# A hybrid decoder trunk: the first LRU input chunk of each layer is worked in two token halves, the first of them between the two halves of V

## The chip, the cores and the metric

The kernel runs on one core of one Trainium2 chip. The metric is the device time in microseconds (us) of one execution; the time before is 1116.06 us, the median of three runs. TensorE (PE) multiplies, VectorE (DVE) and ScalarE (ACT) do the element-wise work, GpSimd (POOL) some small operations and transfers, and SyncE (SP) issues most of the transfers from memory. PEld is TensorE's weight load, which a profile lists apart from the multiplication itself.

## The reference, cut to what matters

There are 256 tokens of width 1024, and two layers. Each layer is

```
h = RMSNorm_pre(x)
[q | k | v | lru_x | lru_gate | glu_in | branch_gates] = h @ w_in
A = dilated attention(q, k, v) @ w_o_attn
B = (RG-LRU(causal_conv4(lru_x)) * gelu(lru_gate)) @ w_o_lru
C = swish(LayerNorm(causal_conv31(GLU(glu_in)))) @ w_o_conv
x += RMSNorm_post((sigmoid-gated sum of A, B, C) @ w_out)
x += RMSNorm_post(relu(RMSNorm_pre(x) @ w_up)^2 @ w_down)
```

All of it is in float32. What the change touches is the product of `h` with 256 of the 1024 columns of `lru_x` (the chunk called lx1) in each layer, and where that product stands beside the product for the first third of V.

## The kernel before, in words

**Weights.** All weights come in chunks of 1 MB (128 partitions x 2048 floats), 92 for each layer, in a fixed order (ORDER and chunk_plan). The function `weights` loads a chunk into a raw buffer (two of them, tag "raw"), then splits it in two pieces of 1024 columns: ACT casts to `whi`, rounded to the type fp32r (line 416), and DVE subtracts to get the rest, `wlo` (line 429). `whi` and `wlo` have three buffers each. The activations are split likewise, into `hh` and `hl`. A product is then three fp32r matmuls for each block of 128 input rows: whi*hh, whi*hl and wlo*hh.

**Two forms of product.** In the form "ws" the weights are the stationary operand (128x128) and the tokens stream past, all 256 of them: `ws_items` makes, for each half j of a chunk and each four blocks k, a list a of eight matmuls (whi) and a list b of four (wlo), that is 48 matmuls of 256 columns for a chunk. In the form "as" the activations are stationary and 512 weight columns stream past; one matmul makes 128 tokens. V is in this form: two chunks (v00, v01), and for each 128 tokens t 12 matmuls of 512 columns for each chunk.

**The start of a layer.** `h` is made in two token halves: `pre_norm(t)` squares and sums on ACT, finds the root, scales on DVE (`xn_mix`), transposes on PE (`pt_mix`, line 483) and splits into `hh_mix` (ACT) and `hl_mix` (DVE). The first entry of ORDER, v0, is therefore taken apart (`vproj` with apart true): first both chunks for the tokens t=0, then both for t=1. The second entry is lx1, the third glu0. At the start of layer 1 the last matmuls of the layer before (`dn`) for t=1 stand between.

**What sets the order.** Every operation is an `Op`; `main` chains all products in the order in which the program makes them, so PE works them in that order, with transposes and the small products of attention put between them. A planner (`Sched.run`) simulates the five engines with a cost for each operation, takes the ready one with the longest way to the end, and fixes the order of the instructions on every engine. For an fp32r matmul the cost it uses is 0.4266 ns for each streamed column. The engines then run their lists in order and wait on each other. PSUM accumulators of the tag "mm" have four places, and each chunk's matmuls wait for their accumulator, for `whi`/`wlo` and for `hh`/`hl`.

**After lx1.** `lx` copies the accumulator (`xp`), makes a causal convolution of four taps over all 256 tokens (`lu`) and splits it; that is used some chunks later by `lru_gates`. The loads of the LRU gate weights (`lwr`, POOL's queue) are ordered behind `starts["lx1"]`.

Of the kernel before, what the change touches and what calls it, by code (L numbers as in the profile page):

```python
# [13 lines left out]
P = 128  # L14
T = 256
# [361 lines left out]
def trunk_kernel(ctx: ExitStack, tc: tile.TileContext, x_d, pos_d, w_d, lruw_d, par_d, gain_d, const_d, id_d, out_d):  # L377
# [5 lines left out]
    S = Sched()  # L383
# [4 lines left out]
    def slot(name, dt=F32, shape=(P, 2, T)):  # L388
        return S.buf(sp, shape, dt, "s2", name, NSLOT)

    def mm_ps(name, shape=(P, 2, T), ring=True):
        return S.buf(pp, shape, F32, "mm", name, 4, ring)
# [55 lines left out]
    def dma(eng, out, in_, nbytes):  # L448
        def fn():
            o = out.ap() if isinstance(out, View) else out  # L450
            i = in_.ap() if isinstance(in_, View) else in_
            eng.dma_start(out=o, in_=i)

        e = {id(nc.gpsimd): "POOL", id(nc.scalar): "ACT"}.get(id(eng), "SP")
        o = S.op(e, DMA_ISSUE[e], fn, views(in_), views(out))
        o.dma = nbytes / DMA_RATE / 1e3
        return o

    def memset(out, v):
        return S.op("POOL", 60 + 0.5 * out.n, lambda: nc.gpsimd.memset(out.ap(), v), [], [out])  # L460

    def matmuls(items):
        cost = 0
        reads, writes, seen = [], [], set()
        for out, lhs, rhs, start, stop in items:
            n = rhs.n
            cost += n * 0.4266 if lhs.buf.dt == F32R else n * 1.69
            for v, l in ((lhs, reads), (rhs, reads), (out, writes)):
                k = (id(v.buf), v.reg, l is writes)
                if k not in seen:  # L470
                    seen.add(k)
                    l.append(v)

        def fn():
            for out, lhs, rhs, start, stop in items:
                nc.tensor.matmul(out.ap(), lhsT=lhs.ap(), rhs=rhs.ap(), start=start, stop=stop)  # L476

        return S.op("PE", cost, fn, reads, writes)
# [8 lines left out]
    last_main = [None]  # L487

    def main(items, *more):
        for it in (items,) + more:  # L490
            o = matmuls(it)
            o.main = True
            if last_main[0] is not None:
                S.follow(last_main[0], o)
            last_main[0] = o
        return o

    def split(hi, lo, src, scale=None):
        if scale is None:
            return act(hi, src, AF.Copy), tt(lo, src, hi.f32(), OP.subtract)  # L500
        return (act(hi, src, AF.Copy, scale=scale),
                stt(lo, src, scale, hi.f32(), OP.mult, OP.subtract))
# [5 lines left out]
    def weights(l, name, spread=False):  # L508
        c = CIDX[name]
        assert c == used[l], (name, c, used[l])  # L510
        used[l] += 1
        nm = f"{name}_{l}"
        raw = S.buf(wp, (P, CHUNK), F32, "raw", f"raw_{nm}", NRAW)
        if l or c:
            o = dma(nc.sync, raw.all(), w_d[l * NCH + c], CHUNK * P * 4)
            if l == 0 and c in late:
                S.follow(o, late[c])
        else:
            for s in range(2):
                o = dma(nc.sync, raw[:, s * HALF:(s + 1) * HALF], w_d[0][:, s * HALF:(s + 1) * HALF], HALF * P * 4)  # L520
                if ORDER[0][0] == "v":
                    S.follow(o, x1_load)
        if spread:
            hs, ls = [], []
            for q in range(4):
                hs.append(slot(f"whi_{nm}{q}", F32R, (P, 512)))
                ls.append(slot(f"wlo_{nm}{q}", F32R, (P, 512)))
                for o in split(hs[q].all(), ls[q].all(), raw[:, q * 512:(q + 1) * 512]):
                    o.prep = True
            return [(Quarters(hs[2 * s:2 * s + 2]), Quarters(ls[2 * s:2 * s + 2])) for s in range(2)]  # L530
        offs = (3 * LINE // 8, LINE // 8) if KIND[name] != "as" else (3 * LINE // 8,) * 2 if name[:2] in ("v1", "v2") else (0, 0)
        hi = Shifted(S.buf(wp, (P, CHUNK + LINE // 2), F32R, "whi", f"whi_{nm}", NHI), offs[0])
        lo = Shifted(S.buf(wp, (P, CHUNK + LINE // 2), F32R, "wlo", f"wlo_{nm}", NHI), offs[1])
        n = HALF if l == 0 and c < 2 else PREP
        for b in range(0, CHUNK, n):
            for o in split(hi[:, b:b + n], lo[:, b:b + n], raw[:, b:b + n]):
                o.prep = True
        return [(Part(hi, s * HALF), Part(lo, s * HALF)) for s in range(2)]
# [30 lines left out]
    def alloc_h(name):  # L569
        hi = [S.buf(sp, (P, 4, T), F32R, "hh", f"hh_{name}_{b}", 2) for b in range(2)]  # L570
        lo = [S.buf(sp, (P, 4, T), F32R, "hl", f"hl_{name}_{b}", 2) for b in range(2)]
        return hi, lo
# [56 lines left out]
    def hk(h, k, sl=slice(None)):  # L629
        return h[0][k // 4][:, k % 4, sl], h[1][k // 4][:, k % 4, sl]  # L630
# [90 lines left out]
    rope_tables()  # L721
    softplus()

    def ws_items(ps, j, w, rhs, nk=8, pitch=P, off=0):
        hi, lo = w
        out = []
        for k0 in range(0, nk, 4):
            a, b = [], []
            for k in range(k0, k0 + 4):
                s = slice(k * pitch + off, k * pitch + off + P)  # L730
                mh, ml = rhs(k)
                a.append((ps[:, j, :], hi[:, s], mh, k == 0, False))
                a.append((ps[:, j, :], hi[:, s], ml, False, False))
                b.append((ps[:, j, :], lo[:, s], mh, False, k == nk - 1))
            out += [a, b]
        return out

    def ws_mm(ps, w, rhs):
        first = last_main[0]
        for j in range(2):  # L740
            main(*ws_items(ps, j, w[j], rhs))

    for l in range(L):
        if l == 0:
            h = h0
        hr = lambda k, h=h: hk(h, k)
# [4 lines left out]
            late[6] = last_gain[0]  # L751
        merged = {}
        upad, cacc, taps = {}, {}, {}
        starts = {}

        def gemm(name, w, ps, rhs):
            n0 = len(S.ops)
            ws_mm(ps, w, rhs)
            starts[name] = S.ops[n0]

        def p1(buf, i):
            return buf[:, l, i:i + 1]
# [44 lines left out]
        lu, luh, lul, lru = {}, {}, {}, {}  # L807

        def lx(j):
            w = weights(l, f"lx{j}")  # L810
            ps = mm_ps(f"lx{j}_{l}")
            gemm(f"lx{j}", w, ps, hr)
            xp = S.buf(sp, (P, 2, 260), F32, "xp", f"xp{j}_{l}", 2)
            memset(xp[:, :, 0:3], 0.0)
            act(xp[:, :, 3:3 + T], ps.all(), AF.Copy)
            u = slot(f"lu{j}_{l}")
            for s in range(2):
                i = 2 * j + s
                act(u[:, s, :], ps[:, s, :], AF.Identity, scale=p1(par, CW + 24 + i), bias=p1(par, CB + i))
            for k in range(3):  # L820
                for s in range(2):
                    i = 2 * j + s
                    stt(u[:, s, :], xp[:, s, k:k + T], p1(par, CW + k * 8 + i), u[:, s, :], OP.mult, OP.add)
            lu[j] = u
            luh[j] = slot(f"luh{j}_{l}", F32R)
            lul[j] = slot(f"lul{j}_{l}", F32R)
            split(luh[j].all(), lul[j].all(), u.all())
# [83 lines left out]
        def vproj(g, apart):  # L911
            acc = [mm_ps(f"v{g}{t}_{l}", (P, 512)) for t in range(2)]
            src = lambda kk, t: hk(h, kk, slice(t, T, 2) if g else slice(t * P, (t + 1) * P))
            ws = [weights(l, f"v{g}0")] + ([weights(l, f"v{g}1")] if apart else [])

            def part(kb, t):
                if len(ws) <= kb:
                    ws.append(weights(l, f"v{g}{kb}"))
                for q in range(2):
                    m = main(as_items(acc, ws[kb][q], src, (4 * kb + 2 * q, 4 * kb + 2 * q + 1), 7, t))  # L920
                    starts.setdefault(f"v{g}", m)

            for t in ((0,), (1,)) if apart else ((0, 1),):
                for kb in range(2):
                    part(kb, t)
            for t in range(2):
                vt[g, t] = slot(f"vt{g}{t}_{l}", shape=(P, 512))
                act(vt[g, t].all(), acc[t].all(), AF.Copy)
# [160 lines left out]
        mh, ml = {}, {}  # L1089
# [23 lines left out]
        for name in ORDER:  # L1113
            kind, a = name[:2], name[2:]
# [39 lines left out]
        h = alloc_h(f"mlp{l}")  # L1154
# [30 lines left out]
        hr = lambda k, h=h: hk(h, k)  # L1185
# [37 lines left out]
        for kb in range(1, 8):  # L1223
# [4 lines left out]
            for c in range(2):  # L1228
                w = weights(l, f"dn{kb - 1}{c}", HOLD and kb == 7 and c == 1 and l + 1 < L)
# [7 lines left out]
        if l + 1 < L:  # L1237
            h = alloc_h(f"mix{l + 1}")
# [108 lines left out]
```

## Time and profile before

| | |
|---|---|
| median of three runs | 1116.06 us (1115.8 to 1116.9) |
| the profiled execution | 1113.95 us, of which the span of the trace is 1112.2 us |
| matmuls | 8258 |
| DVE, ACT, POOL busy | 81%, 65%, 6% of the span |
| granted TensorE clock, mean | 0.999 |
| memory traffic | 201.08 MB read, 182 GB/s over the span |

In the rows below all times are in us from the start of the span, unless marked ns. A row of the timeline gives the start, the length, the engine, the line, the operation with output and inputs, the shapes and a count; in brackets stands the idle time before it with what ended that. Matmuls overlap in the pipeline: the record of one is longer than the distance to the next one, and the distance from start to start is what a matmul costs in a stream. Where a row holds x4, its length is three distances and one record.

### The profile page before, as it was taken

To read this page: it belongs to the slowest core of one execution; us is meant where nothing else is said; L and a number is where in the kernel's file an instruction comes from. 1 tells how busy PE (TensorE), PEld (TensorE's weight loads), DVE (VectorE), ACT (ScalarE), POOL (GpSimd) and SP (SyncE) were. 2 spreads that over 40 slices of the span, in tenths; PEclk is the share of its full clock that TensorE was granted. 3 is DMA by queue.
4 is the path that set the end of the run, shared out by engine and by line. 5 is a ranking of instruction groups with operands and counts; after the bars stand their busy time and mean duration, and the time that the engine had idled before them with its cause. 6 is when DMAs were issued, how large, how long until landed. Compare 5 with 4: busy or idle time off the path is not lost.

```text
span 1112.2 us, 20605 instructions
## 1 busy us (share of the span) xinstructions
PE 1095.9 (99%) x8258; PEld 1023.9 (92%) x8258; DVE 902.4 (81%) x1380; ACT 727.7 (65%) x1186; POOL 70.1 (6%) x156
## 2 busy tenths in 40 slices
PE   7999999999999999999999999999999999999997
PEld 6999999998899899989889999999988998998996
DVE  6999999999969865555679999999996889655554
ACT  5879948787775454444569896569676746444443
POOL 1000022111000110000000000221200001000000
PEclk9999999999999999999999999999999999999999
DMA  8664466554436565555555553764633364555551
GB/s 294 247 208 152 152 226 236 184 193 149 142 121 245 195 211 197 194 194 189 189 200 215 181 182 116 255 222 171 216 123 143 146 248 161 214 190 189 194 190 71
DMA packets 37650, 209.77 MB, mean 189 GB/s; under 512 B 6449, under 2 KB 9777, under 8 KB 14130
## 3 DMA queue, kind: packets, MB, share of 16 engines
q1 hardware_dynamic: 32976, 200.05, 50.9%
q0 software_dynamic: 4576, 8.40, 2.3%
q8 instruction: 65, 1.06, 0.4%
q14 instruction: 31, 0.25, 0.1%
q10 hardware_dynamic: 2, 0.00, 0.0%
HBM read 201.08 MB, written 1.05 MB: 182 GB/s over the span
## 4 chain that ended last, share of the span: by engine, by line
PE 82%; DVE 10%; ACT 4%; DMA 2%; issue 1%; SPq 0%; DVEq 0%; ACTq 0%
PE dn L476 15%; PE up L476 14%; PE glu L476 8%; PE v L476 6%; PE ga L476 4%; PE gc L476 4%; PE wo L476 4%; PE oc L476 4%; PE lx L476 3%; PE k L476 3%; PE q L476 3%; PE lg L476 2%; PE ob L476 2%; PE ua L476 2%; PE oa L476 2%; PE pv L476 1%
## 5 line engine op out<-in xcount | busy, mean ns | idle before, releaser
L429 DVE TENSOR_TENSOR wlo_dn<-raw_dn,whi_dn 128x1024 fp32r<-128x1024 f32 (+1 forms) x66 | 76.7, 1190 | 71.2 <-ACT whi_dn L416 71.2
L416 ACT CAST whi_dn<-raw_dn 128x1024 fp32r<-128x1024 f32 (+1 forms) x66 | 65.4, 1023 | 78.9 <-PE dn L476 41.0
L433 DVE SCALAR_TENSOR_TENSOR c<-upad,parh,c 128x256 f32<-128x256 f32 x256 | 110.6, 477 | 0.1
L476 PE MATMUL up<-hl_mlp,whi_up 128*128 128x256 f32 x448 | 107.9, 277 | 0.0
L476 PE MATMUL up<-hh_mlp,whi_up 128*128 128x256 f32 x448 | 107.9, 277 | 0.0
L429 DVE TENSOR_TENSOR wlo_up<-raw_up,whi_up 128x1024 fp32r<-128x1024 f32 x56 | 67.3, 1222 | 48.2 <-ACT whi_up L416 48.2
L476 PE MATMUL dn<-whi_dn,uh 128*128 128x512 f32 x256 | 99.8, 390 | 0.0
L476 PE MATMUL dn<-wlo_dn,uh 128*128 128x512 f32 x256 | 99.8, 390 | 0.0
L423 ACT ACTIVATE cpd<-upad,parh 128x256 f32<-128x256 f32 x224 | 95.3, 499 | 5.7 <-DVE c L429 5.1
L416 ACT CAST whi_up<-raw_up 128x1024 fp32r<-128x1024 f32 x56 | 57.1, 1047 | 51.7 <-PE dn L476 25.4
L476 PEld LDWEIGHTS up<-hh_mlp,whi_up 128*128 128x128 f32 x448 | 84.1, 188 | 0.5
L476 PEld LDWEIGHTS up<-hl_mlp,whi_up 128*128 128x128 f32 x448 | 84.1, 188 | 0.5
L476 PE MATMUL dn<-whi_dn,ul 128*128 128x512 f32 x256 | 70.0, 389 | 0.0
L476 PE MATMUL up<-hh_mlp,wlo_up 128*128 128x256 f32 x448 | 69.4, 277 | 0.0
L429 DVE TENSOR_TENSOR cpd<-cpd 128x1024 f32<-128x1024 f32 (+2 forms) x84 | 63.0, 773 | 0.3 <-ACT cpd L423 0.3
L476 PE MATMUL glu<-hh_mix,whi_glu 128*128 128x256 f32 x256 | 61.2, 276 | 0.0
L476 PE MATMUL glu<-hl_mix,whi_glu 128*128 128x256 f32 x256 | 61.2, 276 | 0.0
L476 PEld LDWEIGHTS up<-hh_mlp,wlo_up 128*128 128x128 f32 x448 | 59.4, 188 | 0.0
L476 PEld LDWEIGHTS dn<-whi_dn,ul 128*128 128x128 f32 x256 | 48.1, 188 | 10.0
L476 PEld LDWEIGHTS dn<-wlo_dn,uh 128*128 128x128 f32 x256 | 48.1, 188 | 9.6
L476 PEld LDWEIGHTS dn<-whi_dn,uh 128*128 128x128 f32 x256 | 48.1, 188 | 9.5
L476 PEld LDWEIGHTS glu<-hl_mix,whi_glu 128*128 128x128 f32 x256 | 48.1, 188 | 0.0
(309 smaller groups left out, 3446.6 us busy)
## 6 DMA issues: line engine op xcount, KB each, us to landing
raw_dn<-w_in_stream SPq DMA_DIRECT2D x32, 1024.0 KB, 4.8
raw_up<-w_in_stream SPq DMA_DIRECT2D x28, 1024.0 KB, 4.8
raw_glu<-w_in_stream SPq DMA_DIRECT2D x16, 1024.0 KB, 4.9
raw_q<-w_in_stream SPq DMA_DIRECT2D x12, 1024.0 KB, 5.0
raw_k<-w_in_stream SPq DMA_DIRECT2D x12, 1024.0 KB, 4.8
raw_v<-w_in_stream SPq DMA_DIRECT2D x11, 1024.0 KB, 4.9
raw_lx<-w_in_stream SPq DMA_DIRECT2D x8, 1024.0 KB, 4.8
raw_lg<-w_in_stream SPq DMA_DIRECT2D x8, 1024.0 KB, 4.8
```

Of the source, the lines that this page charges most:

```text
L416: nc.scalar.copy(out.ap(), in_.ap())
L423: nc.scalar.activation(out.ap(), in_.ap(), func, scale=val(scale), **kw)
L429: lambda: nc.vector.tensor_tensor(out=out.ap(), in0=a.ap(), in1=b.ap(), op=op), [a, b], [out])
L433: lambda: nc.vector.scalar_tensor_tensor(out=out.ap(), in0=a.ap(), scalar=val(s), in1=b.ap(), op0=op0, op1=op1), [a, b] + views(s), [out])
L476: nc.tensor.matmul(out.ap(), lhsT=lhs.ap(), rhs=rhs.ap(), start=start, stop=stop)
```

## The change: what it does

`ws_items` takes a range of token columns, `cols`. A new function, `ws_part`, makes the products of a chunk for the 128 tokens of half t only: the same 48 matmuls (24 for each j), each with 128 streamed columns in place of 256. In `vproj`, when v0 is taken apart, the weights and the accumulator of lx1 are fetched after the V matmuls for t=0, and `ws_part` for t=0 is put there; the V matmuls for t=1 follow. Where `lx(1)` stood, `ws_part` for t=1 takes the place of the whole product, into the same accumulator. `starts["lx1"]` is now the first operation of the first half. The order of the chunks in memory and of their loads stays. The planner's cost of a matmul of 128 columns is half that of one of 256.

```diff
--- before.py
+++ after.py
@@ -721,7 +721,7 @@
     rope_tables()
     softplus()
 
-    def ws_items(ps, j, w, rhs, nk=8, pitch=P, off=0):
+    def ws_items(ps, j, w, rhs, nk=8, pitch=P, off=0, cols=slice(0, T)):
         hi, lo = w
         out = []
         for k0 in range(0, nk, 4):
@@ -729,16 +729,20 @@
             for k in range(k0, k0 + 4):
                 s = slice(k * pitch + off, k * pitch + off + P)
                 mh, ml = rhs(k)
-                a.append((ps[:, j, :], hi[:, s], mh, k == 0, False))
-                a.append((ps[:, j, :], hi[:, s], ml, False, False))
-                b.append((ps[:, j, :], lo[:, s], mh, False, k == nk - 1))
+                a.append((ps[:, j, cols], hi[:, s], mh, k == 0, False))
+                a.append((ps[:, j, cols], hi[:, s], ml, False, False))
+                b.append((ps[:, j, cols], lo[:, s], mh, False, k == nk - 1))
             out += [a, b]
         return out
 
     def ws_mm(ps, w, rhs):
-        first = last_main[0]
         for j in range(2):
             main(*ws_items(ps, j, w[j], rhs))
+
+    def ws_part(ps, w, h, t):
+        cols = slice(t * P, (t + 1) * P)
+        for j in range(2):
+            main(*ws_items(ps, j, w[j], lambda k: hk(h, k, cols), cols=cols))
 
     for l in range(L):
         if l == 0:
@@ -751,7 +755,7 @@
             late[6] = last_gain[0]
         merged = {}
         upad, cacc, taps = {}, {}, {}
-        starts = {}
+        starts, ahead = {}, {}
 
         def gemm(name, w, ps, rhs):
             n0 = len(S.ops)
@@ -807,9 +811,13 @@
         lu, luh, lul, lru = {}, {}, {}, {}
 
         def lx(j):
-            w = weights(l, f"lx{j}")
-            ps = mm_ps(f"lx{j}_{l}")
-            gemm(f"lx{j}", w, ps, hr)
+            if f"lx{j}" in ahead:
+                w, ps = ahead[f"lx{j}"]
+                ws_part(ps, w, h, 1)
+            else:
+                w = weights(l, f"lx{j}")
+                ps = mm_ps(f"lx{j}_{l}")
+                gemm(f"lx{j}", w, ps, hr)
             xp = S.buf(sp, (P, 2, 260), F32, "xp", f"xp{j}_{l}", 2)
             memset(xp[:, :, 0:3], 0.0)
             act(xp[:, :, 3:3 + T], ps.all(), AF.Copy)
@@ -923,6 +931,11 @@
             for t in ((0,), (1,)) if apart else ((0, 1),):
                 for kb in range(2):
                     part(kb, t)
+                if t == (0,):
+                    ahead["lx1"] = weights(l, "lx1"), mm_ps(f"lx1_{l}")
+                    n0 = len(S.ops)
+                    ws_part(ahead["lx1"][1], ahead["lx1"][0], h, 0)
+                    starts["lx1"] = S.ops[n0]
             for t in range(2):
                 vt[g, t] = slot(f"vt{g}{t}_{l}", shape=(P, 512))
                 act(vt[g, t].all(), acc[t].all(), AF.Copy)
```

## Rows read from the trace of the kernel before

**Rows 1.** The page: busy time by engine, and the granted clock in 40 slices.
```profile
PE 1095.9 (99%) x8258; PEld 1023.9 (92%) x8258; DVE 902.4 (81%) x1380; ACT 727.7 (65%) x1186; POOL 70.1 (6%) x156
...
PEclk9999999999999999999999999999999999999999
```
**Rows 2.** The chain that ended last, in order of time: start, us, what.
```profile
16.55 8.20 PE v L476 x36
24.74 5.47 PE lx L476 x48
...
566.18 5.82 PE v L476 x24
572.00 5.47 PE lx L476 x48
```
**Rows 3.** Timeline of PE, start of layer 1.
```profile
559.87 0.73 PE L476 MATMUL v<-whi_v,hl_mix 128*128 128x512 f32 x2 [0.32 <-DVE hl_mix L429]
...
564.09 0.61 PE L476 MATMUL v<-whi_v,hl_mix 128*128 128x512 f32 x2
564.88 1.29 PE L483 MATMUL pt_mix<-ident,xn_mix 128*128 128x128 f32 x8 [0.17 <-DVE xn_mix L433]
```
**Rows 4.** Instructions of tile lx: duration ns min/median/max, first and last start.
```profile
L476 PEld LDWEIGHTS lx<-hh_mix,whi_lx x128: 187/188/188, 24.4 to 636.4; 128*128 128x128 f32 x128
L476 PE MATMUL lx<-hh_mix,whi_lx x128: 276/276/280, 24.6 to 636.5; 128*128 128x256 f32 x128
```
**Rows 5.** Timeline of PEld and PE (last row: by tile, ns): short matmuls with 128-column loads.
```profile
311.78 0.53 PEld L476 LDWEIGHTS var<-ones,vars 128*128 128x128 f32 x4
311.90 0.50 PE L476 MATMUL var<-ones,vars 128*128 128x1 f32 x4
...
556.21 0.60 PE L483 MATMUL pt_mix<-ident,xn_mix 128*128 128x128 f32 x4
...
L483 PE MATMUL pt_mix<-ident,xn_mix x32: 270/273/475, 7.1 to 565.9; 128*128 128x128 f32 x32
```
**Rows 6.** Instructions by tile: weight loads of 32 and of 64 columns.
```profile
L476 PEld LDWEIGHTS mup<-c,ones x32: 106/108/109, 296.5 to 849.2; 128*32 128x32 f32 x32
...
L476 PEld LDWEIGHTS pv<-pT,vt x192: 132/137/137, 266.6 to 847.2; 128*64 128x64 f32 x192
```
**Rows 7.** Timeline of layer 0 by engine: end of V for t=0, and lx1's weights.
```profile
18.69 0.61 PE L476 MATMUL v<-whi_v,hl_mix 128*128 128x512 f32 x2
...
17.49 1.98 ACT L416 CAST whi_lx<-raw_lx 128x1024 fp32r<-128x1024 f32 x2
...
18.71 0.28 DVE L690 CAST rt_r<-posi 128x256 f32<-128x256 int32 x1
...
19.29 2.29 DVE L429 TENSOR_TENSOR wlo_lx<-raw_lx,whi_lx 128x1024 fp32r<-128x1024 f32 x2
```
**Rows 8.** Timeline of DVE, layer 1: weights of lx1 and of glu0.
```profile
565.31 1.22 DVE L429 TENSOR_TENSOR wlo_lx<-raw_lx,whi_lx 128x1024 fp32r<-128x1024 f32 x1
...
570.40 2.36 DVE L429 TENSOR_TENSOR wlo_glu<-raw_glu,whi_glu 128x1024 fp32r<-128x1024 f32 x2 [2.67 <-ACT whi_glu L416]
```
**Rows 9.** Waits of PE, whole span: us in total, times, longest.
```profile
PE sc L476 <- DVE mx L972: 2.2, 2, 1.4
...
PE tp L483 <- ACT sm L423: 0.5, 1, 0.5
PE psi L476 <- ACT lu L423: 0.5, 2, 0.3
```
**Rows 10.** Instructions of tile rt_r: rope-table operations on DVE in layer 0.
```profile
L433 DVE SCALAR_TENSOR_TENSOR rt_r<-rt_nh,rt_r x6: 415/418/419, 32.4 to 58.5; 128x256 f32<-128x256 f32 x6
```
**Rows 11.** Timeline of PE: the attention product, with 64-column loads.
```profile
266.59 1.96 PE L476 MATMUL pv<-pT,vt 128*64 128x256 f32 x24
```
**Rows 12.** Instructions of tile mu: a matmul of plain f32.
```profile
L476 PE MATMUL mu<-mus,ones x4: 377/378/378, 302.9 to 851.4; 128*128 128x256 f32 x4
```
**Rows 13.** Timeline of PE, layer 0: V just after the engine's first work.
```profile
12.23 1.05 PE L476 MATMUL v<-whi_v,hl_mix 128*128 128x512 f32 x2
```

## The prediction

> **What bounds the kernel now.** I read the busy times first: TensorE is busy for 1095.9 of 1112.2 us, and no other engine comes near [rows 1]. So an instruction more on TensorE is paid in full unless it fills time in which TensorE waited. Then I read the chain that ended last around the two places of the change. In layer 0 it is TensorE's own: 36 V matmuls in 8.20 us (0.228 us each) and then the 48 of lx1 in 5.47 us (0.114 each) [rows 2]. In layer 1 it is the same pair, behind the norm of the last tokens [rows 2]. The third view is TensorE's timeline at the start of layer 1, for what the change could win. The reader is to see how little idle time there is. The last two V matmuls for t=0 start at 564.09, so TensorE could take the next instruction at 564.09 + 2 x 0.228 = 564.55. The eight transposes of the other token half start at 564.88, since xn_mix was late: 0.33 us lost [rows 3]. At 0.11 us each (worked out below) they are through at 565.75, and V for t=1 starts at 566.18 [rows 2], when the split of the transposed half is there: 0.43 us lost. That is 0.76 us in all, and the 0.32 us before them [rows 3] lie inside V for t=0, ahead of what is moved. In layer 0 V runs from t=0 into t=1 in one stretch of 36 matmuls without a break [rows 2]: there is nothing to win.
>
> **The price of the split.** The change keeps the number of streamed columns (48 x 256 = 2 x 48 x 128) and doubles the matmuls: 96 for lx1 in each layer, each with its own weight load, 96 more in the whole program. So everything hangs on the distance between two fp32r matmuls of 128 columns with 128x128 loads, and no row has one. I bound it from both sides.
>
> From below: if only the columns counted, half of 0.114, that is 0.057 us, and the split would cost nothing. From above: if a matmul this short were worked like plain f32. The plain f32 matmul of 256 columns has two instructions to a matmul, and each record is 378 ns [rows 12] where one of fp32r is 276 [rows 4]; the 102 ns more are about another 256 columns at 0.114 us. So a plain f32 matmul streams each column four times, and 128 columns would take 4 x 0.057 = 0.228 us.
>
> Nearest lies a third figure, the weight load. A load's record grows with its columns: 108 ns for 32, 137 for 64 [rows 6], 188 for 128 [rows 4], that is 80 ns for (188 - 108) / 96 = 0.83 ns a column, in which 128 columns take 107 ns. That this is a rate and not only a delay is seen where matmuls are too short to cover it. The var matmuls stream one column each, yet their four loads stand in 0.53 us, (0.53 - 0.19) / 3 = 0.113 us apart [rows 5]; the matmuls follow at the same distance. The transposes have 128 columns and 128-column loads, as the new matmuls will, and four stand in 0.60 us with a record of 0.273: (0.60 - 0.273) / 3 = 0.109 us [rows 5]. So at 256 columns load and stream just balance, and at 128 the load sets the pace. I take 0.114 us, what lx has today: 96 x 0.114 = 10.94 us for lx1 in place of 5.47, so **+5.47 us in each layer, +10.9 us in all**.
>
> The Trainium skill speaks of this distance too ("TensorE: Matmul & The Clock Gate", section "Back-to-back issue gap"): a sustained stream of load and matmul pairs is given there as about 81 ns a matmul at 128 columns. By that the cost would be 96 x 0.081 - 5.47 = 2.3 us a layer. The same sentence gives about 131 ns at 512 columns, where this trace has 228 [rows 2], so I don't follow it here.
>
> **What the change wins or waits for, layer 1.** Half of lx1 now covers the time until hh_mix and hl_mix for t=1 are there, 5.47 us against the 1.6 us from 564.55 to 566.18; V for t=1 will not wait. The transposes still have to stand among the lx1 matmuls; if they are put a list too early, TensorE waits for xn_mix as now. I take 0.6 of the 0.76 us. lx1's own weights are late next: its second j needs the last wlo_lx piece after 24 + 8 matmuls, at 564.55 + 32 x 0.114 = 568.2, and that piece ends at 565.31 + 1.22 = 566.53 even where it stands today [rows 8]. If it moves ahead of the norm on DVE, the norm is later by 1.2 us, inside the cover of 5.47.
>
> **Layer 0.** V for t=0 ends at 18.69 + 2 x 0.228 = 19.15 [rows 7], and lx1 starts 5.4 us earlier than before. Its first eight matmuls need whi_lx alone, whose first half is ready at 18.5; they end at 20.06. The next four need the first half of wlo_lx, which today starts at 19.29 and ends at about 20.45 [rows 7]: a wait of 0.4 us. It is in nobody's way but TensorE's, behind it are V for t=1 and all the rest. The planner may put that subtraction ahead of the conversion at 18.71 and the small operations behind it, and the wait goes; if it stays behind the other split, it is up to 1 us. I take 0.4.
>
> **What else moves.** No transfer is added. glu0's weights need the buffers of v00, which come free after the first twelve V matmuls for t=1, now 5.47 us later. Until glu0 starts there are twelve V matmuls and half of lx1, 2.7 + 5.5 us as before, so the 4.7 us between the end of wlo_glu (570.40 + 2.36 = 572.76) and glu0's start at 572.00 + 5.47 = 577.47 remain [rows 2, 8]. The raw loads behind it on SP's queue shift with TensorE. The lwr loads on POOL's queue are only ordered behind an earlier operation, and are needed after further chunks. The accumulator of lx1 is held for some 11 us more; of the four places two are V's. I cost these at nothing; the cover is that 4.7 us.
>
> **What is given back later.** TensorE's 5.47 us more at the start of layer 0 are time in which DVE can do rope-table work; six such operations of 0.42 us, 2.5 us, stand later, between 32 and 59 [rows 10]. The waits of TensorE for DVE and ACT later come to 2.2 + 0.5 + 0.5 = 3.2 us in both layers [rows 9]. In layer 1 DVE has no such work to bring forward: its preparation is tied to weight buffers that TensorE frees later too. I take 1.0 us given back, in layer 0; bounds 0 and 3.2.
>
> **The sum.** 10.9 - 0.6 + 0.4 - 1.0 = +9.7 us. Against the profiled execution that is 1113.95 + 9.7 = 1123.7; its span is 1112.2, with 1.75 us around it that the change leaves alone. The median of the runs lies 2.1 us above that execution, so I forecast 1116.06 + 9.7 = **1125.8 us**. Its own range is 1123 to 1128.5: the give-back and the layer 0 wait between their bounds, and about 1 us for another order of everything behind.
>
> **The rivals.**
> Not slower: the load hides. If the loads of 128 columns can be taken closer together in a stream of fp32r than var's and the transposes show, so that the columns alone set the pace, the split costs nothing and 0.6 - 0.4 us are won: 1115.9. For it speaks that lx's loads overlap in the record (188 ns each at a distance of 114) [rows 4]; against it that the loads of var stand no closer than 113 [rows 5]. It decides from a distance of 0.068 us downwards: there 2 x (96 x 0.068 - 5.47) = 2.1 us, the 0.2% (2.2 us) that a measurement of this kernel can tell from no change. Chance 8%.
> A distance between: attention's pv matmuls, with loads of 64 columns, stand 1.96 / 24 = 0.08 us apart [rows 11]. At that pace it is 2 x (96 x 0.08 - 5.47) = +4.4, less 0.2: 1120.3. Half as many columns in a load speak against it. Chance 5%; here the page named above would be right.
> More given back: all 3.2 us of waits go, +10.9 - 0.2 - 3.2 = +7.5, or 1123.6; with a luckier order behind it some 2 us less. Chance 12%.
> Plain f32 pace: 2 x (96 x 0.228 - 5.47) = +32.8, less 1.2: 1147.7. Nothing in the trace has an fp32r matmul under 256 columns, so it stays open. Chance 6%.
> A slower clock: in a stretch where TensorE streams half of the time the granted clock could fall. Granted is full speed in all slices [rows 1], but right after the engine's first work the V matmuls take about twice the time (two in 1.05 us, against 0.61 later) [rows 7, 13], as at 1.2 in place of 2.4 GHz. If the 24 V matmuls for t=1 ran so, 24 x 0.2 = 4.8 us a layer: 1135. The transposes and attention's short matmuls stand without that, so 3%.
>
> **How the numbers follow.** The forecast has 66%. The range 1119.5 to 1131 holds it, the larger give-back and the distance between, 83%; the rest lies outside. Faster by over 0.2% needs the load hidden and a lucky order: 3%. Within 0.2%: 5%. Slower: 92%.
>
> **What would show it.** Right: 96 lx1 matmuls of 128 columns in each layer with a distance of 0.11 us, each half some 5.5 us long; in layer 1 no idle time ahead of V for t=1; glu0 later by 5.5 to 6 us in layer 0 and about 5 in layer 1, and the rest unchanged. Wrong: a distance of 0.06 or of 0.23 us; halves of 2.7 us; V for t=1 at twice its time; or a shift at glu0 that has gone by the end of the attention.

## The result, and the profile after

The changed kernel takes 1133.71 us (median of four, 1129.01 to 1136.72) against 1116.48 for the kernel before, in four executions beside it; the ratio is 1.014, with an interval of 1.0117 to 1.0163, or 13 to 18 us more. Forecast were 1125.8 us and a range up to 1131. The direction was right, the size was not. One execution of the kernel under "The planner's price" below, 1861.75 us at a mean granted clock of 0.558, is left out of every number.

The profiled execution is the fastest of the four, 1129.01 us with a span of 1127.0, 14.8 more than before. Its page has 96 matmuls more and 12 us more of busy TensorE, as answers to [rows 1]:

```profile
PE 1107.9 (98%) x8354; PEld 1035.8 (92%) x8354; DVE 903.9 (80%) x1380; ACT 726.0 (64%) x1184; POOL 70.4 (6%) x156
```

The chain that ended last at the start of layer 0 of the changed kernel (start, us, what; answers to [rows 2]):

```profile
11.98 7.01 DMA raw_lx<-w_in_stream
...
19.01 1.05 ACT whi_lx L416
...
20.09 1.24 DVE wlo_lx L429
...
21.37 4.68 PE lx L476 x40
26.05 5.52 PE v L476 x24
31.57 5.31 PE lx L476 x48
36.88 23.21 PE glu L476 x204
```

Each half of lx1 is about as long as the whole was: 48 matmuls in 5.31 us, 0.111 us each. And the chain now runs through the transfer of lx1's weights and their split, which were hidden before. The chain at the start of layer 1:

```profile
572.08 4.86 PE lx L476 x44
576.94 0.90 PE pt_mix L483 x8
577.84 0.40 PE lx L476 x4
578.24 5.58 PE v L476 x24
583.82 5.31 PE lx L476 x48
589.13 10.97 PE glu L476 x96
```

There is no idle time ahead of V for t=1 any more: the transposes stand inside the first half. The waits of TensorE that are new or grown (us in total, times, longest; answers to [rows 9]):

```profile
PE sc L476 <- DVE mx L985: 5.2, 2, 3.3
...
PE lx L476 <- ACT whi_lx L416: 1.1, 1, 1.1
```

For the experiments I cut each trace in four: from the first V matmul to the first of glu0 in each layer, where the change lies, and the rest of each layer. All numbers are differences of starts in the timeline, in us.

| trace | mean granted clock | V to glu0, layer 0 | rest of layer 0 | V to glu0, layer 1 | rest of layer 1 |
|---|---|---|---|---|---|
| before, ahead of the prediction | 0.999 | 20.04 | 528.3 | 18.93 | 534.9 |
| before, e8_before | 0.997 | 20.29 | 533.0 | 18.95 | 538.0 |
| before, f4_before | 0.998 | 20.04 | 529.3 | 18.93 | 535.3 |
| changed, first | 0.998 | 27.21 | 529.1 | 23.21 | 538.0 |
| changed, e0_again | 0.998 | 27.81 | 531.9 | 23.19 | 536.2 |
| changed, f1_look | 0.992 | 32.18 | 533.3 | 23.23 | 535.3 |
| changed, f2_look | 0.996 | 26.15 | 531.4 | 23.20 | 536.8 |
| changed, f3_look | 0.999 | 26.17 | 529.5 | 23.20 | 535.3 |
| e1_inplace | 0.996 | 25.41 | 531.6 | 24.13 | 536.8 |
| e2_layer0 | 0.994 | 32.97 | 529.8 | 18.94 | 537.9 |
| e3_layer1 | 0.998 | 20.31 | 533.9 | 23.20 | 534.3 |
| e5_narrow_loads | 0.997 | 22.95 | 531.7 | 19.02 | 537.1 |
| e6_stationary | 0.996 | 24.82 | 530.0 | 19.23 | 539.0 |
| e7_early_weights | 0.995 | 26.91 | 534.3 | 18.94 | 536.4 |
| e9_stationary_l1 | 0.996 | 20.39 | 532.3 | 19.23 | 539.7 |
| e10_later | 0.999 | 25.47 | 530.0 | 18.94 | 536.8 |

### The profile page after: what moved, and what is told of

The parts are those of the page before. It is cut to its first block, busy times and chain, and to the rows that moved or that the text cites. A ratio compares the mean times of both kernels' runs of the same rounds, so it can differ in the third digit from the quotient of the medians.

```text
span 1127.0 us, 20797 instructions
## 1 busy us (share of the span) xinstructions
PE 1107.9 (98%) x8354; PEld 1035.8 (92%) x8354; DVE 903.9 (80%) x1380; ACT 726.0 (64%) x1184; POOL 70.4 (6%) x156
## 4 chain that ended last, share of the span: by engine, by line
PE 90%; DVE 4%; DMA 2%; ACT 2%; issue 1%; SPq 0%; DVEq 0%; ACTq 0%
PE dn L476 15%; PE up L476 14%; PE glu L476 8%; PE v L476 5%; PE q L476 5%; PE k L476 4%; PE ga L476 4%; PE gc L476 4%; PE lg L476 4%; PE wo L476 4%; PE oc L476 4%; PE lx L476 3%; PE ob L476 3%; PE gb L476 2%; PE ua L476 2%; PE oa L476 2%
```

## The experiments

Theory A: the doubled weight loads cost 5.2 us a layer wherever the halves stand; the rest is the wait for lx1's weights in layer 0, and a stretch at half clock (a granted clock of 1.2 GHz in place of 2.4) that follows it in some executions. The rivals: moving lx1 past V costs by itself; the plan, made with half the price of the matmuls, is bad; the waits at the score products are new; or the halves lower the clock by themselves. Where an expectation gives theories letters, they stand for what it says there. Each ratio is against executions of the kernel before beside that run. Of the diffs only the lines that matter are shown; "..." stands for the others.

**The split without the move.**

```diff
 def lx(j):
-    if f"lx{j}" in ahead:
-        w, ps = ahead[f"lx{j}"]
+    if j == 1:
+        w = weights(l, "lx1")
+        ps = mm_ps(f"lx1_{l}")
...
+        ws_part(ps, w, h, 0)
         ws_part(ps, w, h, 1)
...
-    if t == (0,):
-        ahead["lx1"] = weights(l, "lx1"), mm_ps(f"lx1_{l}")
...
```

> The split alone: lx1 in two halves of 128 tokens in each layer, both where lx1 stood, behind V for t=1. Theory A (the weight load sets a step of 0.112 us): 96 x 0.112 - 5.47 = 5.3 us more in each layer, glu0 later by 5.3 in both, no wait for lx1's weights in layer 0, the 0.76 us ahead of V in layer 1 stay: +10.5 us, 1127 with the clock as in the kernel before, up to 1134 if the score product waits for 3 us again and the clock falls. Theory B (moving lx1 past V is what costs, the split little): within 3 us of the kernel before.

Measured: 1128.14 us, 1.0081 (1.0055 to 1.0106) of the kernel before. V to glu0 is longer by 5.37 us in layer 0 and by 5.20 in layer 1 (25.41 and 24.13 in the table, against 20.04 and 18.93). That is theory A: 10.6 us are the split, and moving alone is no explanation.

**The change in one layer alone** (`if t == (0,) and l == 0` or `l == 1`).

> The change in layer 0 alone. Theory A (each layer pays by itself): +6.7 us at glu0 of layer 0, of which 5.2 are the split and 1.4 the wait for lx1's weights; all of it is still there at the end, and layer 1 waits 1.4 us at the score product as before: 1122.5 to 1124, clock 0.998 or more. Theory B (the sum is more than its parts, since another plan moves the score waits): over 1126 or under 1120.

> The change in layer 1 alone. Theory A: +4.3 us at glu0 of layer 1 (5.2 less the idle time ahead of V), then the same 3 us wait at the score product with the clock at half behind it, another 2 to 5 us: 1122 to 1126, clock below 0.999. Theory B (the long wait comes from both layers together): +4.3 to +5 in all, 1120.5 to 1121.5, wait at the score product 1.4 us, clock 0.999.

Layer 1 alone: 1122.30 us, 1.0031 (1.0007 to 1.0055), V to glu0 +4.27, which is the split less 0.93 us of idle time; its time lies in theory A's bounds, but its longest wait at a score product is 1.4 us, as theory B has it, and the stretch at half clock in its trace stands in layer 0, which this kernel leaves as it was, behind a wait of 4.05 us at an LRU gate. So that part of A's expectation failed. Layer 0 alone: 1129.21 us, 1.0087 (1.0055 to 1.0119), over theory A's 1124 and in theory B's bounds, more than the split and a wait give. The excess lies in the changed place itself, V to glu0 32.97, and not later in the layer, where theory B had looked for it. The first matmul of lx1 there, and the windows behind it (stretch, length, busy PE and count, granted clock, DMA share, GB/s):

```profile
20.65 0.33 PE L476 MATMUL lx<-hh_mix,whi_lx 128*128 128x128 f32 x1 [1.76 <-ACT whi_lx L416]
```

```profile
22.00:23.00 1.00, 1.00 (x9) 0.87 0.54 229
23.00:24.00 1.00, 1.00 (x6) 0.50 0.36 123
...
32.00:33.00 1.00, 1.00 (x4) 0.51 0.00 0
33.00:34.00 1.00, 1.00 (x6) 1.00 0.00 0
```

For 10 us the granted clock is at the lower of its two levels, 1.2 GHz in place of 2.4. TensorE had waited 1.76 us for whi_lx just before (from 18.89 to 20.65). The rest of lx1's first half and the start of V for t=1 run at half speed, some 5 us more.

**The changed kernel again.**

> The changed kernel once more, for its spread and a second trace. Theory A (a long wait lowers the clock): the 3.3 us that TensorE waits at a score product in layer 1 let the granted clock fall to half for some 4 us; executions that are slower have the same instructions and more such stretches, each behind a wait for the scores. So 1129 to 1137 us, mean granted clock 0.991 to 0.998, and every stretch below full speed begins at a wait. Theory B (the half-empty stream lowers the clock): the stretches below full speed lie in or right behind the lx1 halves, where TensorE streams half of the time. Theory C: the spread is memory traffic, the clock stays at 0.998 and the waits for transfers differ.

Measured: 1131.24 us, 1.0115 (1.0076 to 1.0153), mean clocks 0.991 to 0.998. Its trace was one of 0.998, with a single stretch of some 3.4 us at half clock behind a wait of 3.1 us at a score product. It told the theories apart no further, hence the looks below.

**The planner's price** (`cost += max(n, 256) * 0.4266` for fp32r).

> The change with the planner told what a 128-column matmul costs (as much as one of 256 columns). Theory A (the cost is paid on TensorE, whatever the plan says): no more than 2 us from the changed kernel, 1129 to 1134. Theory B (the plan, made with half the price, puts the score products too early, and that costs the rest beyond the split): 1125 to 1127, waits at the score products in sum back to 2.2 us.

Measured: 1132.5 us over five executions, 1.0122 (1.0101 to 1.0143). No trace of it is read. The time is theory A's and says that the plan is not the cause.

**Half the load.**

```diff
-            main(*ws_items(ps, j, w[j], lambda k: hk(h, k, cols), cols=cols))
...
+                    s = slice(k * P, k * P + 64)
...
+                        a.append((ps[0:64, j, cols], w[j][0][:, s], mh, False, False))
...
```

> The changed kernel with most of lx1's weight loads cut to 64 of their 128 columns (22 of 24 matmuls in each list; half of the products of lx1 are left out, the matmuls stay as many and stream 128 columns as before). Theory A (the weight load sets the distance): 64 columns load in about 53 ns and the streamed columns take the same, so the distance falls from 0.112 to 0.06 us or a little more, each half of lx1 from 5.3 to about 3.1 us, and the time by 4 x 2.2 = 9 us. Theory B (an instruction of this kind has a floor of 0.11 us whatever it loads): distance and time stay.

Measured: 1122.11 us, 1.0047 (1.0025 to 1.0069). In the timeline the distance is 0.06 us:

```profile
21.27 0.22 PE L476 MATMUL lx<-hh_mix,whi_lx 128*64 128x128 f32 x1
21.33 0.22 PE L476 MATMUL lx<-hl_mix,whi_lx 128*64 128x128 f32 x1
21.39 0.22 PE L476 MATMUL lx<-hh_mix,whi_lx 128*64 128x128 f32 x1
```

A half that waits for nothing takes 3.05 us. There is no floor of 0.11 us. The edit halves the output rows along with the loads, so this run by itself doesn't part the two; the var matmuls of [rows 5], with full loads and one streamed column at 0.113 us, speak for the load. With both, the price of the split is that of its loads.

**The same halves, loaded the other way round.** The activations are the stationary operand and 256 weight columns stream, so no matmul is doubled; two transposes turn each half.

```diff
-        for j in range(2):
-            main(*ws_items(ps, j, w[j], lambda k: hk(h, k, cols), cols=cols))
...
+                a.append((acc.all(), mh, chunk(hi, k), k == 0, False))
...
+  act(sb.all(), acc.all(), AF.Copy)
+  transposes([(ps[:, j, t * P:(t + 1) * P], sb[:, j, :]) for j in range(2)])
```

> The same place and the same tokens, but lx1's halves with the activations as the stationary operand and 256 weight columns streamed: 24 matmuls of 256 columns for each half, 48 in all as before the change, and two transposes and a copy for each half. Theory A (the doubled loads are the price, and a half-empty stream behind a wait keeps the clock low): the halves take 24 x 0.113 = 2.7 us each, glu0 of layer 0 is later by the wait for lx1's weights alone (1 to 2 us) and that of layer 1 not later; 1116.5 to 1119.5, and no stretch of 10 us at half clock in layer 0 although the wait is the same. Theory B (moving lx1 past V costs by itself): 1121 or more.

> Halves of lx1 with the activations stationary and 256 weight columns streamed, in layer 1 alone, where lx1's weights are there in time. Theory A: four more transposes (0.4 us) against the idle time ahead of V (0.76 us, of which most goes): within 1 us of the kernel before, 0.997 to 1.002 of it. Theory B (bringing lx1 forward costs by itself): 3 us or more over it.

Both layers: 1124.77 us, 1.0054 (1.0035 to 1.0074), about 7 us less than the changed kernel, yet more than theory A's 1116.5 to 1119.5 and in theory B's bounds. The trace has the reason in layer 0, and it is not the move itself: the wait was 1.93 us, and the clock fell here too, but for 3.4 us (the matmul behind the wait, two of those at half clock, 0.21 us apart, and windows as above):

```profile
20.60 0.38 PE L476 MATMUL lxa<-whi_lx,hh_mix 128*128 128x256 f32 x1 [1.93 <-ACT whi_lx L416]
...
23.07 0.41 PE L476 MATMUL lxa<-whi_lx,hh_mix 128*128 128x256 f32 x1
23.28 0.41 PE L476 MATMUL lxa<-whi_lx,hl_mix 128*128 128x256 f32 x1
```

```profile
21.00:22.00 1.00, 0.77 (x7) 0.85 0.68 270
22.00:23.00 1.00, 0.95 (x4) 0.50 0.35 131
...
24.00:25.00 1.00, 1.00 (x7) 0.50 0.94 393
25.00:26.00 1.00, 1.00 (x7) 0.94 0.97 410
```

Behind the wait at the same place the clock was back after 3.4 us where matmuls of 256 columns ran, and after 10 in e2_layer0, where those of 128 did; with one trace here, that the columns make this difference is not shown. Layer 1 alone: 1119.81 us, 1.0021 (1.0002 to 1.0041), V to glu0 +0.30: the transposes and 0.4 us of waiting for xn_mix ate the gain. The ratio lies just over theory A's 1.002, and V to glu0 speaks for A: bringing lx1 forward by itself costs next to nothing there. It is no faster than the kernel before; whether it is slower is at the edge of what was measured.

**Layer 0 with the weights earlier, or lx1's half later.** Both have the change in layer 0 alone. In the one the `lwr` loads go to SP's queue behind glu's; in the other the first half stands behind the first twelve V matmuls for t=1.

```diff
-            S.follow(starts[f"lx{max(j, 1)}"], dma(nc.gpsimd, raw.all(), lruw_d[4 * l + j], 512 * P * 4))
+            if l == 0 and j < 2:
+                S.follow(starts["glu0"], dma(nc.sync, raw.all(), lruw_d[j], 512 * P * 4))
...
```

```diff
-                if t == (0,):
...
+                    if t == (1,) and kb == 0 and l == 0:
...
```

> The change in layer 0 alone, with two loads of 256 KB (the LRU gate weights) moved off POOL's queue to behind glu's on SP's, so that lx1's weights arrive sooner. Theory A (the wait of 1.1 to 1.8 us for lx1's weights both costs itself and starts the stretch at half clock): the wait is 0.4 us or less, glu0 later by 5.5 to 6 us, the mean granted clock 0.996 or more in every execution, 1122 to 1125 in the median against 1129 without the move. Theory B (the half-empty stream lowers the clock by itself): 1128 and clocks under 0.995 remain. If the transfer isn't sooner, nothing is told apart.

> The change in layer 0 alone, with the first half of lx1 one V chunk later (behind twelve of the 24 V matmuls for t=1), so that lx1's weights have 2.7 us more to arrive. Theory A (of what the change costs in layer 0, 5.2 us are the doubled loads, and the rest is the wait for the weights and the stretch at half clock behind it): the wait is under 0.3 us, no stretch at half clock in lx1's halves, glu0 later by 5.2 us: 5 to 6.5 us over the kernel before, mean clock as there. Theory B (half-empty streaming lowers the clock by itself): still 9 us or more over it, with a stretch at half clock in the halves.

The first told little: the transfer still took 6.7 us and the wait was 0.8; 1125.79 us, clocks from 0.993 to 1.0. The second is clear: 1124.16 us, 1.0063 (1.0043 to 1.0083), ten clocks of 0.997 to 0.999. Its chain has no wait in layer 0:

```profile
15.88 5.60 PE v L476 x24
21.48 5.31 PE lx L476 x48
26.79 2.78 PE v L476 x12
29.56 5.31 PE lx L476 x48
34.87 27.29 PE glu L476 x240
```

V to glu0 is 25.47, +5.43, the split and nothing else; the whole time, 7 us over the kernel before, is a little over theory A's 6.5, and the surplus lies behind glu0. The halves alone don't lower the clock: here they ran for 10.6 us with the granted clock at full speed, as in e1_inplace. With e2_layer0 this is the closest pair: the same halves in layer 0, with the wait and without it, at 1.0087 and 1.0063.

**More looks at both kernels.**

> The kernel before once more, for a second trace: 1114 to 1120 us. Theory A: waits for the score products of 1.4 us or less and clock 0.999, or, if it is over 1119, a stretch at half clock behind a score product. Theory C (the waits at the score products differ from one execution to the next as much in the kernel before as in the changed one): 4 us or more of such waits in sum here too.

> A third trace of the changed kernel. Theory A (a wait for lx1's weights in layer 0 and a half-empty stream behind it keep the clock at half for some 10 us in a part of the executions): where the mean clock is 0.995 or less, a stretch at half clock of 8 to 11 us in or behind lx1's first half in layer 0, with V's start to glu0 at 32 to 33 us in place of 27.2. Theory D (stretches behind score products alone): V to glu0 27 to 28 us whatever the clock is, and two or more stretches of 4 us later.

> A fourth trace, as the third: with theory A, V to glu0 in layer 0 is 32 to 33 us where the mean clock is 0.995 or less, with theory D 27 to 28 us in every trace.

> A fifth trace, as the third: with theory A, V to glu0 in layer 0 is 32 to 33 us where the mean clock is 0.995 or less, with theory D 27 to 28 us in every trace.

> A third trace of the kernel before: V to glu0 20.0 to 20.3 us in layer 0 and 18.9 in layer 1, as in the two there are, and what is left of the layers between 528 and 534 us (layer 0) and 534 and 538 us (layer 1), that is, the spread of the rest is not the change's. If its rest lies over 540 or under 526, two traces were too few to say so.

e8_before came out at 1121.41 us with 4.1 us of waits at the score products and a wait of 2.6 us at an LRU gate, just under the 4.2 to 5.9 us at score products in the changed kernel: waits nearly as long come without the change, as theory C has it. f1_look (1135.35 us) is the execution that was missing, V to glu0 32.18. Its windows, and the first matmuls behind the fall (0.21 us apart):

```profile
22.00:23.00 1.00, 1.00 (x11) 1.00 0.39 164
23.00:24.00 1.00, 1.00 (x7) 0.53 1.04 164
...
33.00:34.00 1.00, 1.00 (x5) 0.85 0.00 0
34.00:35.00 1.00, 1.00 (x6) 1.00 0.00 0
```

```profile
20.03 0.33 PE L476 MATMUL lx<-hh_mix,whi_lx 128*128 128x128 f32 x1 [1.19 <-ACT whi_lx L416]
...
23.15 0.41 PE L476 MATMUL lx<-hh_mix,whi_lx 128*128 128x128 f32 x1
23.37 0.41 PE L476 MATMUL lx<-hl_mix,whi_lx 128*128 128x128 f32 x1
```

f3_look is the other end, 1126.05 us, clock 0.999. What separates the two is the transfer of lx1's weights (its issue in SP's timeline, and the row of issues: KB, us to landing). In f3_look:

```profile
12.36 0.33 SPq L452 DMA_DIRECT2D raw_lx<-w_in_stream  x1
raw_lx<-w_in_stream SPq DMA_DIRECT2D x1, 1024.0 KB, 4.8
```

in f1_look:

```profile
11.77 0.33 SPq L452 DMA_DIRECT2D raw_lx<-w_in_stream  x1
raw_lx<-w_in_stream SPq DMA_DIRECT2D x1, 1024.0 KB, 7.1
```

and in the kernel before, e8_before, where lx1 comes 5 us later and nobody waits for it:

```profile
11.86 0.33 SPq L452 DMA_DIRECT2D raw_lx<-w_in_stream  x1
raw_lx<-w_in_stream SPq DMA_DIRECT2D x1, 1024.0 KB, 7.3
```

The earlier issue landed later. It is so in all sixteen traces of the table: issued at 12.3 to 12.8, the transfer took 4.7 to 4.9 us (four traces, the one ahead of the prediction among them); issued at 11.6 to 12.0, it took 6.5 to 7.6 (twelve). No run moved the issue, so why is open.

f2_look had 4.7 us and no wait for whi_lx; its clock of 0.996 comes from two stretches behind score products, the longest wait there 2.5 us. Theory D, with 27 to 28 us in every trace, failed in all three. So theory A as written (0.995 or less, then 32 to 33 us) held in f1_look, and neither f2_look nor f3_look, at 0.996 and 0.999, speaks against it; but the mean clock alone doesn't tell the place, since e7_early_weights has 0.995 from a stretch behind a score product, with 26.91 us from V to glu0. f4_before came as expected, but the rest of layer 0 in e3_layer1 and e7_early_weights (533.9 and 534.3) shows that the spread reaches at least to there.

## Why the prediction was wrong

**The price of the split: right.** Forecast were 5.47 us a layer from the weight load's distance of 0.114; measured 5.37 and 5.20 (e1_inplace), at 0.111. With half the load the distance nearly halved. The Trainium skill's figure of about 81 ns ("TensorE: Matmul & The Clock Gate", "Back-to-back issue gap") did not hold here: 111 ns. The same page of the Trainium skill says, in "Weight-path perf modes — Fast Weight Load (FWL) and DoubleRow", that the fast weight load is on only for input types other than FP32; the rows here print the loads as f32, but no run turned that mode on or off.

**The idle time of layer 1: right, a little small.** Forecast were 0.6 us saved; 5.20 - 4.27 = 0.93 went.

**The step that failed first: the wait in layer 0.** The prediction took 0.4 us, "up to 1", with whi_lx's first half ready at 18.5. That was read off one execution in which the transfer took 4.8 us, the rarer case; the term priced a wait for wlo_lx alone and took the transfer as landed. In other executions of either kernel the same transfer takes 6.5 to 7.6 us, and the split starts at 18.5 to 19.6. Before the change 5 us of V hid this; the change took away just that cover, and the wait became 1.1 to 1.9 us in five of the nine traces with the half in this place (the first, e0_again, f1_look, e2_layer0 and e6_stationary), and 0.77 and 0.95 in e7_early_weights and e5_narrow_loads. In f2_look and f3_look, with a transfer of 4.7 and 4.8 us, only 0.3 and 0.4 for wlo_lx remained, and V to glu0 was +6.1, near the 5.9 of the sum. f3_look against f4_before, spans of 1124.0 and 1113.0, is +11.0: the forecast without its give-back, 10.9 - 0.6 + 0.4 = 10.7. So the sum held where the transfer was short.

**The step that failed worst: the slower clock.** It stood among the rivals with 3%, as a fall that half-empty streaming makes and that V for t=1 pays. In f1_look and e2_layer0 it happened, but otherwise: it came behind the wait of 1.2 to 1.8 us, and the halves themselves, whose matmuls then take 0.213 us, paid about half of it in f1_look and two thirds in e2_layer0, V for t=1 the rest. It costs 5 us (32.18 in f1_look against 27.21 in the first trace with about the same wait). I had argued that short matmuls elsewhere run at full clock; e1_inplace and e10_later show that the halves do so too where no wait stands before them. What the argument lacked was the wait. Not every wait does it: 1.1 us in the first trace and 1.72 in e0_again left the clock at full speed in this place, and what decides is not shown. How often it happens, the traces don't say: once in five of the changed kernel. The mean clock is 0.9944 over its ten timed executions and 0.9948 over the eight of e2_layer0, against 0.9978 (e1_inplace, 12), 0.9981 (e3_layer1, 12), 0.9972 (e9_stationary_l1, 12) and 0.9983 (e10_later, 10), where no half stands behind a long wait, and 0.9978 to 0.9981 in the kernel before. But this mean also counts the stretches behind score products and LRU gates: in the five traces of the changed kernel these cost about 1.7, 1.7, 3.4, 3.4 and 0 us, in the three of the kernel before 0, 1.7 and 0 (estimates, from the granted clock of windows of 1 us). So how much of the fall lies in the changed place stays open.

**The give-back: not seen.** Forecast was 1.0 us; the rest of layer 0 is 529 to 533 us in the changed kernel and 528 to 533 before, a spread in which 1 us would be lost. No run shows the term.

**The score products: not shown to be the change's.** In the first comparison they looked like a new cost, 5.2 us against 2.2. But the kernel before has 2.2, 4.1 and 2.7 us there in its three traces, the changed one 5.2, 5.9, 5.8, 4.9 and 4.2. All five lie above the three. Yet the rest of layer 1 is no longer than before, and both rests together are 1064.8 to 1068.6 us in the changed kernel and 1063.2 to 1071.0 before. A small share may be the change's; these few traces don't settle it.

**What stays open.** From V to glu0 the two layers together are longer by 6.1 + 4.3 = 10.4 us in f3_look, 7.77 + 4.26 = 12.0 in e0_again and 12.1 + 4.3 = 16.4 in f1_look; the medians of the two comparisons, +17.2 and +14.4, lie around the upper end. The clock accounts for most of the spread: the ten executions run from 1129.01 us at 0.998 to 1136.72 at 0.991, 7.7 us, where 0.7% of 1130 us would be 7.9. By the same estimate 0.9978 to 0.9944 is 3.8 us in the mean, and with the 10.4 to 12.0 us without a fall that makes 14 to 16 us; the two ratios, 1.0140 and 1.0115, are 15.6 and 12.8. The sum closes within what was measured, but three of the four executions of the first comparison had clocks of 0.991 to 0.994, and none of them has a trace: in which place they lost their time is not known.

## What to carry to other kernels

Splitting a matmul's streamed columns does not split its price where the weight load already takes as long as the stream: count loads, not columns. If the tokens must be halved, making them the stationary operand was the cheaper form here (V to glu0 of layer 1 +0.30 us in place of +4.27). When work is moved ahead, what its inputs' arrival was hidden by goes too; price the exposed transfer from several executions, since one shows only one of its durations. And ask of each new wait of a microsecond or two what runs behind it, because the clock may fall there, as it did behind three of the five waits of 1.1 to 1.9 us at lx1.

## What was not expected of the hardware

A 1 MB transfer issued at about 12 us, in the same order of instructions, landed after 4.7 to 4.9 us where it was issued at 12.3 us or later and after 6.5 to 7.6 where it was issued at 12.0 or earlier, sixteen traces without an exception. The two lwr loads issued behind it went the same way (4.7 to 5.5 us against 6.2 to 7.1). At the 1.2 GHz level an fp32r matmul of 128 columns takes 0.213 us, as one of 256 columns does at that level in e6_stationary; at full speed they take 0.111 and 0.113. The clock once fallen stayed at 1.2 GHz for some 10 us in the two traces where the halves of 128 columns ran, and rose 3 to 5 us into V; in the one where matmuls of 256 columns followed the wait it was back after 3.4.
